# Splitting streamed weights 1024 columns at a time, into two wide pairs of tiles

## The chip, the cores and the metric

The kernel runs on one core of one Trainium2 chip. The metric is the device time of one execution in microseconds (us). Lower is better. The kernel before has a median of 2492.58 us over three runs (2488.17 to 2494.41).

## The reference

Two layers of a decoder trunk on 512 tokens of width 1024, all in float32. Each layer computes, from the RMS-normed input, one wide input projection whose columns feed three branches, merges the branches by gates, and adds a feed-forward:

```python
def hybrid_layer(x, ...):
    xn = rmsnorm(x, norm1_g)
    proj = xn @ w_in                              # 1024 x 9568
    (ssd_z, ssd_xbc, ssd_dt, mla_cq, mla_ckv, mla_kr, gdn_qkv, gdn_z, gdn_b, gdn_a,
     gate_logits) = jnp.split(proj, split_at, axis=-1)
    y_ssd = ssd_mixer(ssd_z, ssd_xbc, ssd_dt, ...)           # conv, chunked scan, gated norm
    y_mla = mla_mixer(mla_cq, mla_ckv, mla_kr, cos, sin, ...)  # 8 heads, low-rank q and kv
    y_gdn = gdn_mixer(gdn_qkv, gdn_z, gdn_b, gdn_a, ...)     # conv, gated delta rule
    g_ssd, g_mla, g_gdn = jnp.split(jax.nn.sigmoid(gate_logits), 3, axis=-1)
    mixed = g_ssd * (y_ssd @ w_ssd_out) + g_mla * (y_mla @ w_mla_out) + g_gdn * (y_gdn @ w_gdn_out)
    h = x + mixed @ w_out
    f = jnp.square(jax.nn.relu(rmsnorm(h, norm2_g) @ w_up)) @ w_down    # 1024 -> 4096 -> 1024
    return h + f
```

A final RMSNorm follows the second layer.

## The kernel before, in words

Each dense product is computed from parts. A float32 operand is split into a high part (rounded to the reduced format `fp32r`) and a low part, the exact rest; a product is three matmuls, high x high, high x low and low x high (`mm3`, lines 182 to 184). Activations are split once and stay in SBUF (`xh`, `xl`, `yh`, `yl`, `fh`, `fl`, eight tiles of 128 x 512 each). Weights are streamed from HBM and split as they come.

The stream is the generator `weights` (lines 165 to 179). It brings 1024 columns per partition (512 KB) into a raw tile `wraw` of a ring of two, by one DMA on the SyncE queue: two rows of k-tiles of 512 columns, four of 256 or eight of 128. `split_half` (156 to 163) then splits each half, 512 columns: ScalarE copies `raw` to `whi` (line 161), VectorE subtracts `raw - whi` into `wlo` (line 162), both at high priority. `whi` and `wlo` come from the pool `wp`, a ring of four 512-column tiles each; a tile goes back to the ring when its last matmul is done. A caller may pass `hold`, a list of tiles of its own, where all the weights of a product must stay (the second half of the output projection and the last down projection of a layer).

Two functions consume the stream. `dense_F` (186 to 209) makes feature-major products: a weight tile is the stationary operand, 512 tokens move past it, one PSUM bank for each 128 columns of weights. `dense_T` (214 to 249) makes token-major products: an activation tile is stationary and the weights move, one PSUM bank for each of the four token tiles. `dense_F` is called with 256 columns nearly everywhere (gates and branch projections in `out_proj`, convolved channels, the up projection), so a piece of 512 columns is two k-tiles for two banks, 12 matmuls. With `dense_T` at 512 columns a piece is one k-tile for four banks, also 12. With `mid`, `dense_T` uses the first four pieces on half of the tokens before the other half of the norm is done.

In the latent attention (lines 532 to 645), for each of four pairs of heads, the query weights have a stream of their own (`q_weights`, 533 to 548): 384 columns of a k-tile at a time, reordered by two strided copies (544, 545) and two subtractions (546, 547), into the same rings `whi` and `wlo`. The key and value weights of the pair come next as a list: one raw tile, two pieces.

Each engine works through its instructions in an order that a scheduler of the language fixes when the program is built, from priorities and its own estimate of times. It interleaves stages: while the attention or the delta rule waits for a chain of small steps, matmuls of the next dense product stand between them on TensorE. The order of a layer is: query and key/value latents, attention with four pairs of heads, state-space branch in two groups, delta rule (blocks inverted on VectorE, lines 812 to 836; two units, 878 to 987), the three branch projections in between, output projection, feed-forward in four quarters.

Of the kernel before, what the change touches and what calls it, by code (L numbers as in the profile page):

```python
# [59 lines left out]
def hybrid_kernel(ctx, tc, a, out, depth=2, taps=None):  # L60
# [95 lines left out]
    def split_half(raw, hold=None):  # L156
        """The exact high and low parts of 512 columns (or fewer) of raw weights."""
        n = raw.shape[1]
        hi, lo = hold or (mk(wp, [P, n], F32R, "whi"), mk(wp, [P, n], F32R, "wlo"))
        with tc.high_priority():  # L160
            act.copy(hi, raw)  # L161
            dve.tensor_tensor(lo, raw, f32(hi), ALU.subtract)  # L162
        return hi, lo

    def weights(w2d, c0, n, K, hold=None):
        """Yields (k0, hi, lo): split rows of w2d's columns c0 .. c0 + n, some k-tiles at a time.

        hold: the pairs of tiles for 512 columns, where the working ring's are too few.
        """
        kt = min(1024 // n, K // P)  # L170
        step = 512 // n
        for k0 in range(0, K // P, kt):
            raw = mk(wp, [P, kt * n], F32, "wraw", 2)
            sync.dma_start(raw.rearrange("p (k n) -> p k n", n=n),
                           w2d[k0 * P : (k0 + kt) * P, c0 : c0 + n].rearrange("(k p) n -> p k n", p=P))
            for q in range(0, kt, step):
                hi, lo = split_half(raw[:, q * n : (q + step) * n], hold and hold[k0 + q])
                v = lambda x: x.rearrange("p (k n) -> p k n", n=n)
                yield k0 + q, v(hi), v(lo)
# [6 lines left out]
    def dense_F(gen, cols, K, xh, xl, mid=None):  # L186
        """Feature-major products; cols: the slices of the weights' columns, one PSUM bank each.

        mid: called between the two halves of the tokens, which are then computed one after the other.
        """  # L190
        pss = [acc_bank() for _ in cols]
        last = K // P - 1
        if mid:
            gen = list(gen)
            for i, hf in enumerate(HALVES):
                for ps, c in zip(pss, cols):
                    for k0, wh, wl in gen:
                        for k in range(wh.shape[1]):
                            kk = k0 + k
                            mm3(ps[:, hf], wh[:, k, c], wl[:, k, c], xh[kk][:, hf], xl[kk][:, hf], kk == 0, kk == last)  # L200
                if i == 0:
                    mid()
            return pss
        for k0, wh, wl in gen:
            for ps, c in zip(pss, cols):
                for k in range(wh.shape[1]):
                    a_, b_ = wh[:, k, c], wl[:, k, c]
                    mm3(ps[: a_.shape[1], :], a_, b_, xh[k0 + k], xl[k0 + k], k0 + k == 0, k0 + k == last)
        return pss
# [4 lines left out]
    def dense_T(gen, n, K, xh, xl, evac, cols=lambda w: w, mid=None, hook=None):  # L214
        """Token-major products of n columns, one token tile a PSUM bank.

        mid: called after the first weights' products of the first half of the tokens.
        hook: the weights are all held; tokens go tile by tile, hook(t) is called after each tile's.
        """
        pss = [acc_bank()[:, :n] for _ in range(T)]  # L220
        last = K // P - 1

        def part(w, ts):
            k0, wh, wl = w
            for t in ts:
                tok = slice(t * P, (t + 1) * P)
                for k in range(wh.shape[1]):
                    kk = k0 + k
                    mm3(pss[t], xh[kk][:, tok], xl[kk][:, tok], cols(wh[:, k, :]), cols(wl[:, k, :]), kk == 0, kk == last)

        if hook:
            gen = list(gen)
            for t in range(T):
                for w in gen:
                    part(w, (t,))
                evac(t, pss[t])
                hook(t)
            return
        if mid:
            lead = [next(gen) for _ in range(4)]  # L240
            for w in lead:
                part(w, (0, 1))
            mid()
            for w in lead:
                part(w, (2, 3))
        for w in gen:
            part(w, range(T))
        for t in range(T):
            evac(t, pss[t])
# [32 lines left out]
    def norm_half(i, xs, ssq, gcol, pl, hs, ls):  # L282
        """The normed rows' transposes, split, of half the tokens; xs: token tiles [P, D]."""
# [21 lines left out]
    def small_weights(ly):  # L305
        """The columns k_rope | dt | a | b of w_in."""
        raw = mk(wp, [P, KD * 96], F32, "wraw", 2)
        sync.dma_start(raw, a["w_small"][ly])
        res = []
        for q in range(2):  # L310
            hold = [mk(lp, [P, 384], F32R, "mix", 8) for _ in range(2)]
            hi, lo = split_half(raw[:, q * 384 : (q + 1) * 384], hold)
            res.append((4 * q, hi.rearrange("p (k n) -> p k n", k=4), lo.rearrange("p (k n) -> p k n", k=4)))
        return res
# [17 lines left out]
    for ly in range(depth):  # L332
# [40 lines left out]
        def step_sizes():  # L373
            """Softplus of dt and alpha, decays, beta."""
            # softplus of dt and alpha: max(v, 0) + log1p(exp(-|v|))
# [43 lines left out]
        def cum_rows(pl):  # L419
            """Of each token tile's running sums of g: W [row, t, m] and M [row, t, i, l], such that the product over  # L420
            the rows of one group of four heads is the difference of the sums at l and at m of its head i.

            Rows 0 .. 63 pair ones with the sums' high and low parts at l, rows 64 .. 127 the negated parts at m
            with ones.
            """
# [26 lines left out]
        def seg_exp(pl, o, t, h0):  # L452
            """o[m, i, l] = exp(min(sum of g over m < k <= l, 0)) of heads h0 .. h0 + 3, for m <= l; else at most 1."""
# [27 lines left out]
        def latent(tok, width, gi, nm):  # L481
            """RMS-normed latent rows, transposed and split."""
# [22 lines left out]
        def rope(src):  # L505
            """Rotary embedding of the rows of src [P, S], two heads of 64 features."""
# [25 lines left out]
        for hp in range(4):  # L532
            def q_weights():
                for k0 in (0, 2):
# [3 lines left out]
                    for k in range(2):  # L538
                        rv = raw[:, k * 384 : (k + 1) * 384].rearrange("p (h n) -> p h n", h=2)
                        hi = mk(wp, [P, 384], F32R, "whi")  # L540
                        lo = mk(wp, [P, 384], F32R, "wlo")
# [27 lines left out]
            # each head's high part on both halves of the partitions, against the key's high and low parts  # L569
# [21 lines left out]
            for j in range(2):  # L591
# [26 lines left out]
                for kbs in ((0,), (1,), (3, 2)):  # L618
# [11 lines left out]
                    else:  # L630
                        # the first block of columns stays zero
# [18 lines left out]
        def conv_silu(pl, ps, taps_, bias, o):  # L650
            """o = 2 * silu(causal depthwise conv of the rows of ps)."""
# [10 lines left out]
        def silu_T(pl, c0, o):  # L662
            """o[P, T, 512] = 2 * silu of the token-major projection's 512 columns at c0."""
            dense_T(weights(w_in, c0, 512, D), 512, D, xh, xl, lambda t, ps: silu2(o[:, t, :], ps))
# [98 lines left out]
        def key_tiles(c0):  # L763
            """Two key-head tiles of q or k after the convolution."""
# [5 lines left out]
        def gdn_matrix(u):  # L770
            """Per chunk and head, the transpose of -strict(k k^T * decay) * beta."""
# [4 lines left out]
            for t in range(T):  # L776
# [5 lines left out]
                for i in range(2):  # L782
                    # the diagonal holds the squared lengths
# [28 lines left out]
        def gdn_blocks():  # L812
            """The inverses of I minus the 32 x 32 diagonal blocks, one a partition: forward substitution.

            Returns per unit the inverses and their transposes, rows on the partitions of their blocks.
            """
# [21 lines left out]
        def gdn_inverse(nt, xc, yc):  # L838
            """The transposed inverse of I - transpose(nt), by doubling of the diagonal blocks."""
# [38 lines left out]
        def gdn_unit(u, kT, ork, cc, cd, Yt, yh, yl):  # L878
# [35 lines left out]
            for t in range(T):  # L914
# [54 lines left out]
                # q's norm and its 128 ** -0.5 scale the rows of o  # L969
# [68 lines left out]
        def finish(t):  # L1038
            """After the layer's last product of a token tile."""
# [45 lines left out]
def lay_out(inputs):  # L1085
    """The launch's arrays: small parameters side by side, the narrow columns of w_in gathered."""
# [26 lines left out]
```

## Time and profile before

| | |
|---|---|
| median of three runs | 2492.58 us (2488.17 to 2494.41) |
| span of the profiled execution, first to last instruction | 2476.9 us |
| TensorE matmul (PE) busy | 2433.8 us, 98% |
| VectorE (DVE) busy | 1434.1 us, 58% |
| ScalarE (ACT) busy | 1049.5 us, 42% |
| GpSimd (POOL) busy | 54.2 us, 2% |
| copies of line 161 into `whi`, 128x512 | 664, 620 ns each |
| subtractions of line 162 into `wlo`, 128x512 | 664, 689 ns each |
| DMA | 215.17 MB, mean 87 GB/s |

The page gives the profiled execution by its span alone; its own time with what lies around the span isn't shown. PE counts an interval as busy while any matmul is under way, and matmuls overlap, so two starts lie closer together than one matmul lasts. In the rows of the groups the name `acc<-xh,whi` reads: written to `acc`, moving operand `xh`, stationary operand `whi`. The times in a row are the total busy time and the mean of one instruction, then the idle time of its engine just before, with what ended it.

### The profile page before, as it was taken

What the parts mean: (1) busy time and instruction counts of PE and PEld (TensorE: products, weight loads), DVE (VectorE), ACT (ScalarE), POOL (GpSimd) and SP (SyncE); (2) the same over time, 40 slices, a digit from 0 to 9 for tenths busy, and PEclk for the clock granted to TensorE, in tenths of its full rate; (3) what the DMA queues carried; (4) which work ended last, traced back from release to release, by engine and by line L of the source; (5) the groups of instructions that cost most, each with busy time, mean ns of one, the idle gap of its engine ahead of it and who ended that gap; (6) DMA issues with size and microseconds to landing.
All of it is one profiled execution on the core that took longest, in us unless ns stands there. A gap on an engine that the chain in (4) does not pass through costs nothing. (4 is left out here: it accounts for less than half of the span.)

```text
span 2476.9 us, 32227 instructions
## 1 busy us (share of the span) xinstructions
PE 2433.8 (98%) x12164; PEld 1949.4 (79%) x12164; DVE 1434.1 (58%) x2952; ACT 1049.5 (42%) x2189; POOL 54.2 (2%) x70
## 2 busy tenths in 40 slices
PE   7999999999999999999999999999999999999998
PEld 6777787777787888888887777877787878888887
DVE  6776756765675553443557667667656645443444
ACT  5555434434543342332445553444434534422333
POOL 0000000000000000000000000000000000000000
PEclk9999999999999999999999999999999999999999
DMA  4222232342222413223422222223422224222222
GB/s 129 81 60 69 68 86 73 95 114 69 69 68 71 154 64 94 94 94 94 137 74 69 60 77 67 87 69 102 103 77 69 60 77 153 77 94 94 94 94 94
DMA packets 194683, 215.17 MB, mean 87 GB/s; under 512 B 32864, under 2 KB 154208, under 8 KB 194528
## 3 DMA queue, kind: packets, MB, share of 16 engines
q1 hardware_dynamic: 191008, 207.87, 28.2%
q10 hardware_dynamic: 3520, 5.25, 0.9%
q8 instruction: 95, 1.56, 0.3%
q14 instruction: 60, 0.49, 0.1%
HBM read 200.50 MB, written 7.34 MB: 84 GB/s over the span
## 5 line engine op out<-in xcount | busy, mean ns | idle before, releaser
L162 DVE TENSOR_TENSOR wlo<-wraw,whi 128x512 fp32r<-128x512 f32 x664 | 456.6, 689 | 609.2 <-ACT whi L161 598.9
L161 ACT CAST whi<-wraw 128x512 fp32r<-128x512 f32 x664 | 410.6, 620 | 866.4 <-PE acc L183 511.8
L182 PE MATMUL acc<-xh,whi 128*128 128x512 f32 (+1 forms) x1376 | 543.3, 395 | 2.2 <-DVE vl L254 2.2
L183 PE MATMUL acc<-xl,whi 128*128 128x512 f32 (+1 forms) x1376 | 541.3, 394 | 0.0
L184 PE MATMUL acc<-xh,wlo 128*128 128x512 f32 (+1 forms) x1376 | 540.7, 393 | 0.0
L182 PEld LDWEIGHTS acc<-xh,whi 128*128 128x128 f32 x1376 | 258.4, 188 | 58.8 <-DVE vl L254 2.8
L183 PEld LDWEIGHTS acc<-xl,whi 128*128 128x128 f32 x1376 | 258.5, 188 | 57.8 <-issue 1.0
L184 PEld LDWEIGHTS acc<-xh,wlo 128*128 128x128 f32 x1376 | 258.4, 188 | 56.1 <-issue 0.5
L183 PE MATMUL acc<-yl,whi 128*128 128x512 f32 x384 | 154.7, 403 | 0.0
L182 PE MATMUL acc<-yh,whi 128*128 128x512 f32 x384 | 154.4, 405 | 0.0
L184 PE MATMUL acc<-yh,wlo 128*128 128x512 f32 x384 | 154.0, 401 | 0.0
L184 PE MATMUL acc<-whi,xl 128*128 128x512 f32 (+1 forms) x384 | 145.7, 379 | 0.0
L182 PE MATMUL acc<-whi,xh 128*128 128x512 f32 (+1 forms) x384 | 144.8, 379 | 0.0
L183 PE MATMUL acc<-wlo,xh 128*128 128x512 f32 (+1 forms) x384 | 144.7, 377 | 0.0
L659 DVE SCALAR_TENSOR_TENSOR cva<-acc,pc,cva 128x511 f32<-128x511 f32 (+2 forms) x168 | 120.2, 743 | 17.3 <-ACT cva L655 9.9
L182 PE MATMUL acc<-whi,yh 128*128 128x512 f32 x320 | 126.6, 396 | 0.0
L183 PE MATMUL acc<-wlo,yh 128*128 128x512 f32 x320 | 126.6, 396 | 0.0
L184 PE MATMUL acc<-whi,yl 128*128 128x512 f32 x320 | 126.6, 396 | 0.0
L183 PEld LDWEIGHTS acc<-yl,whi 128*128 128x128 f32 x384 | 72.1, 188 | 18.0 <-issue 1.9
L182 PEld LDWEIGHTS acc<-yh,whi 128*128 128x128 f32 x384 | 71.5, 188 | 18.1 <-ACT yh L257 2.3
L184 PEld LDWEIGHTS acc<-yh,wlo 128*128 128x128 f32 x384 | 72.1, 188 | 17.1 <-issue 1.0
L182 PEld LDWEIGHTS acc<-whi,xh 128*128 128x128 f32 x384 | 72.4, 189 | 13.9 <-DVE cva L659 0.5
(335 smaller groups left out, 3912.8 us busy)
## 6 DMA issues: line engine op xcount, KB each, us to landing
wraw<-in_w_in_dram SPq DMA_DIRECT2D x148, 512.0 KB, 3.6
wraw<-in_w_up_dram SPq DMA_DIRECT2D x64, 512.0 KB, 3.6
wraw<-in_w_down_dram SPq DMA_DIRECT2D x64, 512.0 KB, 3.6
wraw<-in_w_mla_out_dram SPq DMA_DIRECT2D x16, 512.0 KB, 3.4
wraw<-in_w_ssd_out_dram SPq DMA_DIRECT2D x16, 512.0 KB, 3.4
wraw<-in_w_gdn_out_dram SPq DMA_DIRECT2D x16, 512.0 KB, 3.4
wraw<-in_w_out_dram SPq DMA_DIRECT2D x16, 512.0 KB, 3.7
wraw<-in_mla_w_uq_dram SPq DMA_DIRECT2D x16, 384.0 KB, 3.3
```

What stands on the lines that cost most here:

```text
L161: act.copy(hi, raw)
L162: dve.tensor_tensor(lo, raw, f32(hi), ALU.subtract)
L182: pe.matmul(o, ah, bh, start=start, stop=False)
L183: pe.matmul(o, ah, bl, start=False, stop=False)
L184: pe.matmul(o, al, bh, start=False, stop=stop)
L659: dve.scalar_tensor_tensor(acc[:, d:], ps[:, : S - d], taps_[3 - d], acc[:, d:], ALU.mult, ALU.add)
```

## The change

A streamed raw tile that is not held is now split whole: one copy and one subtraction of 1024 columns. The ring has two pairs of 1024-column tiles in place of four of 512, the same SBUF. A piece now holds two, four or eight k-tiles, so 24 matmuls. The query weights of the attention keep their pieces of 384 columns, and take them from the same ring, which has two slots now. The key and value weights are one piece. `dense_T` with `mid` takes two pieces ahead in place of four. Held weights are split by 512 as before. Comments and docstrings are gone, with no effect.

```diff
     def split_half(raw, hold=None):
         n = raw.shape[1]
-        hi, lo = hold or (mk(wp, [P, n], F32R, "whi"), mk(wp, [P, n], F32R, "wlo"))
+        hi, lo = hold or (mk(wp, [P, n], F32R, "whi", 2), mk(wp, [P, n], F32R, "wlo", 2))
         with tc.high_priority():
             act.copy(hi, raw)
             dve.tensor_tensor(lo, raw, f32(hi), ALU.subtract)
         return hi, lo
...
         kt = min(1024 // n, K // P)
-        step = 512 // n
+        step = max(512 // n, 1)
         for k0 in range(0, K // P, kt):
             raw = mk(wp, [P, kt * n], F32, "wraw", 2)
             sync.dma_start(raw.rearrange("p (k n) -> p k n", n=n),
                            w2d[k0 * P : (k0 + kt) * P, c0 : c0 + n].rearrange("(k p) n -> p k n", p=P))
+            v = lambda x: x.rearrange("p (k n) -> p k n", n=n)
+            if not hold:
+                hi, lo = split_half(raw)
+                yield k0, v(hi), v(lo)
+                continue
             for q in range(0, kt, step):
-                hi, lo = split_half(raw[:, q * n : (q + step) * n], hold and hold[k0 + q])
-                v = lambda x: x.rearrange("p (k n) -> p k n", n=n)
+                hi, lo = split_half(raw[:, q * n : (q + step) * n], hold[k0 + q])
                 yield k0 + q, v(hi), v(lo)
...
         if mid:
-            lead = [next(gen) for _ in range(4)]
+            lead = [next(gen) for _ in range(2)]
...
             def q_weights():
...
-                        hi = mk(wp, [P, 384], F32R, "whi")
-                        lo = mk(wp, [P, 384], F32R, "wlo")
+                        hi = mk(wp, [P, 384], F32R, "whi", 2)
+                        lo = mk(wp, [P, 384], F32R, "wlo", 2)
```

## The prediction

> **What bounds the kernel now.** I read the page's busy times first, then the windows by stage.
>
> ```profile
> span 2476.9 us, 32227 instructions
> PE 2433.8 (98%) x12164; PEld 1949.4 (79%) x12164; DVE 1434.1 (58%) x2952; ACT 1049.5 (42%) x2189; POOL 54.2 (2%) x70
> ```
>
> ```profile
> core 0: us, PE busy (x) PEld busy (x) DVE busy (x) ACT busy (x) POOL busy (x), PEclk, DMA share, GB/s
> 0.00:62.00 62.00, 49.10 (x290) 42.39 (x291) 38.03 (x93) 36.62 (x87) 4.88 (x15) 1.00 0.43 129
> 62.00:124.00 62.00, 58.65 (x307) 45.91 (x306) 46.43 (x118) 36.62 (x99) 1.01 (x1) 1.00 0.29 81
> 124.00:186.00 62.00, 59.30 (x311) 45.49 (x310) 43.39 (x107) 33.66 (x90) 0.00 (x0) 0.97 0.22 60
> 186.00:930.00 744.00, 739.16 (x3841) 590.56 (x3840) 465.51 (x974) 324.86 (x661) 20.78 (x21) 1.00 0.29 83
> 930.00:1178.00 248.00, 248.00 (x1065) 199.45 (x1064) 101.02 (x155) 76.69 (x130) 0.00 (x0) 1.00 0.30 94
> 1178.00:1302.00 124.00, 122.72 (x633) 102.41 (x632) 64.06 (x132) 55.46 (x127) 4.52 (x8) 1.00 0.33 105
> 1302.00:1426.00 124.00, 118.50 (x614) 90.88 (x612) 85.27 (x216) 68.50 (x184) 0.00 (x0) 0.97 0.24 64
> 1426.00:2418.00 992.00, 986.54 (x4892) 790.42 (x4891) 564.76 (x1118) 400.52 (x783) 20.78 (x21) 1.00 0.30 87
> 2418.00:2477.00 59.00, 51.88 (x225) 41.88 (x224) 25.59 (x45) 16.55 (x36) 2.19 (x4) 0.97 0.26 94
> ```
>
> TensorE (PE) is the bound: 2476.9 - 2433.8 = 43.1 us of the span are not PE. Of these 62 - 49.10 = 12.9 lie in the first window and 59 - 51.88 = 7.1 in the last, where inputs arrive and the output leaves. The other 23 us sit mostly in the latent attention (3.35 + 2.70 in layer 0, 1.28 + 5.50 around it in layer 1). In the feed-forward window 930:1178 PE never idles, and 248.00 / 1065 = 0.233 us is the spacing of its 512-column matmuls. So the change, which shortens ACT and DVE work, can gain at most a part of those 23 us; it can lose wherever a split weight piece now comes late.
>
> Next, what a split costs and when it starts (rows of the groups, shapes apart, then of the waits):
>
> ```profile
> L162 DVE TENSOR_TENSOR wlo<-wraw,whi 128x512 fp32r<-128x512 f32 x664 | 456.6, 689 | 609.2 <-ACT whi L161 598.9 <-PE acc L184 5.6 <-PE sm L686 2.3
> L161 ACT CAST whi<-wraw 128x512 fp32r<-128x512 f32 x664 | 410.6, 620 | 866.4 <-PE acc L183 511.8 <-PE acc L184 315.9 <-DVE tok L826 9.8
> L546 DVE TENSOR_TENSOR wlo<-wraw,whi 128x256 fp32r<-128x256 f32 x32 | 13.4, 419 | 6.2 <-ACT whi L544 6.2
> L544 ACT CAST whi<-wraw 128x256 fp32r<-128x256 f32 x32 | 13.1, 409 | 6.9 <-PE acc L184 5.0 <-PE acc L183 1.1 <-DMA wraw<-in_mla_w_uq_dram 0.5
> L547 DVE TENSOR_TENSOR wlo<-wraw,whi 128x128 fp32r<-128x128 f32 x32 | 9.1, 284 | 0.0
> L545 ACT CAST whi<-wraw 128x128 fp32r<-128x128 f32 x32 | 9.8, 306 | 0.0
> L288 DVE TENSOR_SCALAR xr<-h,nrs 128x1024 f32<-128x1024 f32 x16 | 12.1, 758 | 7.6 <-POOL nrs L262 7.1 <-DMA wraw<-in_w_small_dram 0.4
> ```
>
> ```profile
> ACT whi L161 <- PE acc L183: 511.8, 331, 5.7
> ACT whi L161 <- PE acc L184: 315.9, 157, 3.8
> ```
>
> The copies stand ready and wait for PE to give a slot back (488 of 664 times). The ring is full, and its depth decides how early a piece is ready.
>
> **The change part by part.**
>
> *Fewer, wider splits.* 664 copies and 664 subtractions become 332 of each, 1024 columns wide. No such copy is in the trace. From 256 to 512 columns ACT grows by 0.211 us and DVE by 0.270, so 1024 columns are estimated at 0.620 + 0.422 = 1.04 us on ACT and 0.689 + 0.540 = 1.23 on DVE. Bounds for the subtraction are 0.758 (the one 1024-column DVE row, another operation) and 2 x 0.689 = 1.38; I take 1.23, from the same operation. ACT saves 332 x (1.24 - 1.04) = 66 us, DVE 332 x (1.38 - 1.23) = 49. Both lie beside PE work, so I count them as nothing by themselves. The Trainium skill (Perfetto Trace Analysis, Optimizing Scalar/DVE Operations) gives about 93 ns of access overhead an instruction for ScalarE and 60 for VectorE, by which the savings would be an estimated 31 and 20 us. The same section says that larger operations help an engine that is saturated, and that where an unsaturated one causes bubbles elsewhere, breaking its instructions up lets work finish sooner: this speaks against the change, and DVE's 58% and ACT's 42% put the kernel in its second case.
>
> *A ring of two wide pairs, in the dense stages.* In the feed-forward one old piece feeds 12 matmuls, a wide one 24. An old piece goes into a slot that becomes free three pieces before it is needed, 36 x 0.233 = 8.4 us; a wide one has a single piece, 24 x 0.233 = 5.6 us. What the split takes out of that:
>
> ```profile
> 1001.61 0.62 ACT L161 CAST whi<-wraw 128x512 fp32r<-128x512 f32 x1 [1.93 <-PE acc L183]
> 1002.27 0.69 DVE L162 TENSOR_TENSOR wlo<-wraw,whi 128x512 fp32r<-128x512 f32 x1 [1.78 <-ACT whi L161]
> ```
>
> Copy start to end of subtraction is 1.35 us, so pieces lie ready 8.4 - 1.35 = 7.0 us ahead. After: 1.04 + 1.23 + 0.04 between them = 2.3, so 5.6 - 2.3 = 3.3 us ahead. That is halved but still positive: cost 0. The cover is 3.3 us; what is queued in front on ACT and DVE may take that long and no more. In the built order of the changed program half of the wide pieces have 5.8 us of matmuls or more between the release and the first use, and nine in ten have about 5 or more.
>
> *The query weights of latent attention.* Their pieces are 384 columns, but now share the two slots where there were four. This is the costly edit. One piece feeds 9 matmuls = 2.1 us. Before, all four pieces of a unit of two heads could be split ahead; in the built order no release lay less than 3.9 us of matmuls before the use. Now pieces three and four and the key/value piece behind them (one wide piece, 2.3 us of splitting) each wait for a release about one piece ahead: covers of 0.2 to 3 us are common there. The split itself takes 0.409 + 0.419 + 0.284 = 1.11 us, and other work stands between:
>
> ```profile
> 97.38 0.41 ACT L544 CAST whi<-wraw 128x256 fp32r<-128x256 f32 x1 [0.58 <-PE acc L183]
> 97.69 0.58 ACT L253 CAST kh<-acc 128x512 fp32r<-128x512 f32 x1
> 98.17 0.30 ACT L545 CAST whi<-wraw 128x128 fp32r<-128x128 f32 x1
> ```
>
> With one such operation (0.58) ahead on ACT and a 0.69 one on DVE a piece needs 2.4 us against 2.1: a stall of 0.3. With two more it is 1.5; with none, zero. There are three such waits in each of 4 units x 2 layers = 24. Bounds: 0 and 24 x 1.5 = 36 us. I take 0.5 each, 12 us, and put a third of it into time in which PE idles anyway (the attention windows hold 12.8 us of idle): +8. Behind a waiting copy on ACT stand the exponentials and evictions of the running head, and behind the subtraction the row maxima; PE's next score product waits for them, so a stall is not repaid at once. The raw tiles are freed by these splits too, so SP issues the next query DMA later:
>
> ```profile
> wraw<-in_mla_w_uq_dram SPq DMA_DIRECT2D x16, 384.0 KB, 3.3
> ```
>
> It lands 3.3 us after its issue, inside one attention unit, so this costs nothing unless two splits in a row are late.
>
> *End of the delta rule.* In the built order the first two gate pieces of the last branch projection have their copy on ACT behind work that waits for a matmul only 0.3 to 0.4 us before the first use (3.5 us before the change). The low part is needed after 1.2 and 1.5 us and takes 2.3: 1.1 + 0.8 in each layer, 3.8 us; I take +3, as PE waits there already in part (idle of 4.84 and 5.46 in the long windows).
>
> *Start.* The first query-latent piece is 0.42 longer on ACT and 0.54 on DVE, with PE waiting: +1.
>
> *Earlier banks.* With twice the columns a piece, the first bank of a product ends 12 matmuls before the second in place of 6, and token tiles end six matmuls apart in place of three; evictions and the latent norms start up to 1.4 us sooner. Where PE waits for those, it gains; -1 a layer, -2.
>
> *Nothing.* Held weights (output projection's second half, last down projection) keep their 512-column splits; the lead of two wide pieces in the first product holds the same four k-tiles; semaphores fall in number beside full PE time.
>
> Sum: 8 + 3 + 1 - 2 = +10 us on a span of 2476.9, 2486.9. The page gives no time beyond its span; the median of the runs shown, 2492.6, lies 15.7 us above the span, which I keep: **2503 us**. The change of 0.4% is little above the 0.3% (7.5 us) that a measurement of this kernel can tell from no change.
>
> **The rivals.**
>
> *Faster: relief wins.* 115 us less ACT and DVE work reaches PE where the chains are latency-bound, in the attention windows (DVE 46.43 of 62) and the delta rule. It can take no more than the 23 us of inner idle; if a third goes, and the query pieces find their engines free (zero stalls), -8: 2485. It decides if PE's idle in 62:186 falls below the 6.05 us of now. Against it: that idle is mostly of transfers and of chains with few splits in them.
>
> *No change.* Query stalls fall into gaps already there: 0 to +5, about 2495.
>
> *Slower: convolutions use up the lead.*
>
> ```profile
> L659 DVE SCALAR_TENSOR_TENSOR cva<-acc,pc,cva 128x511 f32<-128x511 f32 x56 | 41.6, 745 | 16.5 <-ACT cva L655 9.9 <-ACT cva L657 6.6
> L266 DVE SCALAR_TENSOR_TENSOR ft<-ft,cva 128x512 f32<-128x512 f32 x56 | 38.2, 688 | 9.4 <-ACT ft L265 8.4
> ```
>
> Each tile brings 3 x 0.745 + 0.688 = 2.9 us to DVE, two tiles 5.8, at the same priority as the splits. If both stand before a subtraction, 5.8 - 3.3 = 2.5 us are lost, 28 pairs of tiles x 2.5 = 70 at worst; at a half, with the rest, 2503 + 35 = 2538. For it: the lead of 7.0 us covered this, 3.3 does not. Against: the split comes at high priority as well, between the tiles.
>
> *Slower: the clock.* The granted clock is 0.97 in 124:186 and in 1302:1426, the two windows with attention's long waits: 0.03 x 62 = 1.9 and 0.03 x 124 = 3.7 us. If the new stalls join old waits into long ones in four more units, at 1.9 to 3.7 each, that is about +11: 2514. The Trainium skill (TensorE: Matmul & The Clock Gate, Why this matters for your kernels) says that an idle window of some 3 us halves the clock; the trace agrees as far as the clock falls only where waits are longest.
>
> **How the numbers follow.** The forecast has 0.43, no change 0.22, faster 0.18, convolutions 0.10, clock 0.07. Of the forecast's own spread (+3 to +25) about 0.05 falls inside 0.3%. So faster 0.18, same 0.27, slower 0.55. The range reaches from the faster case, 2484, over the upper bound of the query stalls with the delta rule (+36 + 1) to 2530; the convolutions at full price and a few microseconds of the faster side are left out.
>
> **What would show it.** Right: 332 copies near 1.04 us and as many subtractions near 1.23; PE idle in the attention windows up by some 4 us a layer, with `acc` matmuls of the query latents waiting for ACT or DVE; 930:1178 still without idle; about 2 us more idle at the end of the delta rule. Wrong: idle in the feed-forward or the convolution stages (the lead is smaller than 3.3), or attention windows with less idle than now (relief), or subtractions far from 1.23.

## The result, and the profile after

The changed kernel takes 2507.0 us in the median (11 runs, 2504.3 to 2513.6), the kernel before 2489.1 beside it (11 runs, 2470.8 to 2505.6): a ratio of 1.0085, 95% interval 1.0061 to 1.0109, slower by 15 to 27 us. (This ratio is not the quotient of the two medians, which is 1.0072.) The profiled execution took 2506.3 us, 1.8 more than its span.

The page after, span and busy times, then the groups of the splits (out<-in, count | busy us, mean ns of one | idle before and what ended it):

```profile
span 2504.5 us, 31169 instructions
...
PE 2447.0 (98%) x12164; PEld 1952.8 (78%) x12164; DVE 1407.5 (56%) x2620; ACT 996.1 (40%) x1857; POOL 54.2 (2%) x70
```

```profile
L162 DVE TENSOR_TENSOR wlo<-wraw,whi 128x1024 fp32r<-128x1024 f32 x332 | 406.2, 1224 | 536.1 <-ACT whi L161 533.6 <-PE acc L186 1.0
```

```profile
L161 ACT CAST whi<-wraw 128x1024 fp32r<-128x1024 f32 x332 | 348.5, 1050 | 734.9 <-PE acc L187 401.4 <-PE acc L188 316.4 <-DMA wraw<-in_w_up_dram 6.9
```

The splits are what was forecast: 332 copies of 1.05 us and 332 subtractions of 1.22. ACT and DVE are less busy by 53 and 27 us, and the kernel is slower.

TensorE's own waits say where (waiting line <- what it waited for: us in total, times, longest); first the changed kernel, then the kernel before, whose lines have numbers lower by four:

```profile
PE sm L608 <- ACT qps L583: 11.4, 6, 3.3
...
PE sm L939 <- DVE tok L936: 4.0, 8, 0.8
PE sm L461 <- DVE sg L459: 3.6, 2, 1.8
...
PE acc L186 <- ACT whi L548: 3.0, 4, 0.9
...
PE acc L186 <- ACT whi L161: 2.1, 2, 1.1
```

```profile
PE sm L604 <- ACT qps L579: 4.6, 4, 2.1
...
PE sm L935 <- DVE tok L932: 1.3, 4, 0.3
```

TensorE hardly waits for a split: 5.1 us, the last two rows. What grew most is the wait of the first rope score product of a pair of heads (L608, L604 before) for `qps`, the rotated query, whose two halves are swapped by a DMA just before ("the swap" below).

The windows by stage show the same (start:end, length, then busy us of PE, PEld, DVE, ACT, POOL, the granted clock, DMA). Both kernels are cut at the same work, to within 0.6 us: the latent attention of a layer from its first rope product to its last value product, then what lies from there to the end of the delta rule ("the middle" below). Before, then after:

```profile
88.50:209.60 121.10, 117.80 (x614) 89.52 (x614) 83.32 (x212) 67.32 (x178) 0.52 (x1) 0.99 0.21 58
209.60:772.20 562.60, 557.98 (x2985) 444.20 (x2983) 373.77 (x807) 251.01 (x513) 18.05 (x16) 1.00 0.29 79
1313.00:1436.90 123.90, 119.56 (x616) 90.47 (x615) 83.19 (x212) 67.68 (x179) 0.52 (x1) 0.97 0.21 57
1436.90:2000.10 563.20, 557.93 (x2984) 444.17 (x2983) 373.82 (x806) 251.02 (x513) 18.05 (x16) 1.00 0.28 79
```

```profile
87.80:220.50 132.70, 125.87 (x625) 94.34 (x625) 84.95 (x210) 67.01 (x175) 0.52 (x1) 0.92 0.21 56
220.50:789.00 568.50, 561.26 (x2987) 445.78 (x2986) 366.78 (x728) 236.66 (x435) 18.04 (x16) 1.00 0.28 78
1330.00:1461.20 131.20, 122.38 (x623) 92.32 (x623) 84.53 (x209) 66.44 (x173) 0.52 (x1) 0.95 0.21 57
1461.20:2028.80 567.60, 559.74 (x2987) 444.67 (x2986) 366.59 (x727) 236.61 (x435) 18.04 (x16) 1.00 0.28 78
```

The attention is longer by 11.6 and 7.3 us (8 in the second layer when it is cut at the products themselves), the middle by 5.9 and 4.4; everything else together is 1.6 shorter. In the attention PE's busy time grew too, by 8.1 and 2.8 us for 11 and 7 matmuls more: the granted clock is 0.92 and 0.95 there, against 0.99 and 0.97.

**Why the clock has to be taken out first.** The two profiled executions differ in their mean granted clock:

```profile
core 0: 2476.9 us, clock 0.997
```

```profile
core 0: 2504.5 us, clock 0.992
```

Each run comes with its span and mean clock. Over 93 runs of the kernel before, clock from 0.981 to 0.998 and span from 2471.4 to 2509.9, the two go together (correlation -0.99): 2.1 us for each 0.001, and 2.0 in the 29 runs beside the first experiments. A microsecond at half clock thus costs about 0.4 (0.5 / 2490 of the mean, times 2000). Below, "at full clock" is the span less 2.0 us for each 0.001 that its clock falls short of 1, averaged over the runs of a kernel (scatter 0.9 to 2.0). The kernel before stands at 2470.9 (2470.5 and 2471.4 beside later experiments) with a mean clock of 0.991 to 0.992, the changed kernel at 2487.7 with 0.991. So 17 us of the difference are not the clock and 0 to 2 are. Of the 27.6 us between the profiles 10 are: the profile of before was one of its runs with the highest clock.

### The profile page after: what moved, and what is told of

Its sections match the earlier page's. It is cut to its first block, busy times and chain, and to the rows that moved or that the text cites. A ratio compares the mean times of both kernels' runs of the same rounds, so it can differ in the third digit from the quotient of the medians.

```text
span 2504.5 us, 31169 instructions
## 1 busy us (share of the span) xinstructions
PE 2447.0 (98%) x12164; PEld 1952.8 (78%) x12164; DVE 1407.5 (56%) x2620; ACT 996.1 (40%) x1857; POOL 54.2 (2%) x70
## 5 line engine op out<-in xcount | busy, mean ns | idle before, releaser
L162 DVE TENSOR_TENSOR wlo<-wraw,whi 128x1024 fp32r<-128x1024 f32 x332 | 406.2, 1224 | 536.1 <-ACT whi L161 533.6
L161 ACT CAST whi<-wraw 128x1024 fp32r<-128x1024 f32 x332 | 348.5, 1050 | 734.9 <-PE acc L187 401.4
```

## The experiments

Times are medians of 12 runs (11 of the changed kernel, 29 to 35 of the one before), with the ratio to the kernel before in the same session; e11 and e12 are single runs.

| kernel | us | ratio, 95% interval | mean clock | at full clock |
|---|---|---|---|---|
| before | 2487.4 to 2490.3 | 1 | 0.991 to 0.992 | 2470.5 to 2471.4 |
| changed | 2507.0 | 1.0085, 1.0061 to 1.0109 | 0.991 | 2487.7 |
| e1, query k-tiles in pairs | 2489.9 | 1.0011, 0.9981 to 1.0040 | 0.994 | 2476.5 |
| e2, changed, splits of 512 | 2504.5 | 1.0050, 1.0022 to 1.0078 | 0.990 | 2483.3 |
| e3, before, two slots for query high parts | 2495.5 | 1.0010, 0.9978 to 1.0042 | 0.992 | 2475.1 |
| e4, changed, no swap | 2493.7 | 1.0020, 0.9992 to 1.0047 | 0.993 | 2478.7 |
| e5, before, no swap | 2496.9 | 1.0036, 1.0009 to 1.0064 | 0.990 | 2475.8 |
| e6, e1 with splits of 512 | 2489.2 | 1.0006, 0.9985 to 1.0027 | 0.993 | 2473.8 |
| e7, e1 with the swap on SyncE | 2480.6 | 0.9974, 0.9951 to 0.9996 | 0.996 | 2471.1 |
| e8, changed, swap on SyncE | 2499.3 | 1.0039, 1.0006 to 1.0073 | 0.993 | 2483.6 |
| e9, before, swap on SyncE | 2484.1 | 0.9977, 0.9949 to 1.0005 | 0.993 | 2467.2 |
| e10, e6 with the swap on SyncE | 2481.9 | 0.9959, 0.9932 to 0.9986 | 0.994 | 2467.2 |
| e11, changed, 3 subtractions in the feed-forward | 2521.2 | | 0.991 | |
| e12, changed, 4 subtractions there | 2587.8 | | 0.983 | |

The first theory was A: with two slots in place of four, the query pieces of the next pair of heads come late; fewer of their matmuls stand ahead of the first rope product, and TensorE waits there. The trace has 29, 30, 35 and 33 matmuls between the last score product of line 603 and the first of line 604 in the four pairs before, and 21, 21, 27 and 32 after. The rival B was the width: a 1024-column subtraction ends later everywhere.

**e1: both k-tiles of a raw tile of query weights in one wide pair.**

```diff
+                    hi = mk(wp, [P, 768], F32R, "whi", 2)
+                    lo = mk(wp, [P, 768], F32R, "wlo", 2)
                     for k in range(2):
-                        hi = mk(wp, [P, 384], F32R, "whi", 2)
-                        lo = mk(wp, [P, 384], F32R, "wlo", 2)
...                      (the same copies and subtractions, into columns k * 384 ..)
-                        yield k0 + k, hi.unsqueeze(1), lo.unsqueeze(1)
+                    yield k0, hi.rearrange("p (k n) -> p k n", k=2), lo.rearrange("p (k n) -> p k n", k=2)
```

> The changed kernel, except that both k-tiles of a raw tile of query weights go into one wide pair (768 of its 1024 columns), so that two pieces hold all four k-tiles of two heads. Theory A (query pieces): in the changed kernel only 21 query matmuls of the next two heads stand between the last k-part score product and the first rope score product of a pair of heads, where the kernel before had 29 to 33 matmuls, because the third and fourth piece wait for a slot; TensorE then waits for the rope chain (the row PE sm <- ACT qps) and the clock is halved behind that wait. With the paired pieces 25 to 32 stand there again. A expects a loss of no more than 8 us against the kernel before (about 2488 to 2497), at most two half-clock stretches in the attention, and attention stages of 122 to 126 us in place of 132.7 and 131.2. Theory B (width: the later end of a 1024-column split costs the time everywhere): the query pieces matter little, 2500 to 2510.

2489.9 us, where A had 2488 to 2497. At full clock 11.2 us of the 17 are back. 25, 32, 31 and 32 matmuls stand ahead of the rope products, and their wait has nearly gone:

```profile
PE sm L608 <- ACT qps L583: 0.9, 3, 0.5
```

**e2: the wide ring, filled by two copies and two subtractions of 512.**

```diff
-            act.copy(hi, raw)
-            dve.tensor_tensor(lo, raw, f32(hi), ALU.subtract)
+            for c in range(0, n, 512):
+                s = slice(c, min(c + 512, n))
+                act.copy(hi[:, s], raw[:, s])
+                dve.tensor_tensor(lo[:, s], raw[:, s], f32(hi[:, s]), ALU.subtract)
```

> The changed kernel, except that a wide tile is filled by two copies and two subtractions of 512 columns in place of one of each; ring and slots are those of the change. Theory A (slots of the query weights): the ring is unchanged, so the query matmuls ahead of the rope products stay at 21 and the loss stays: 2500 to 2510, attention stages of 129 to 134 us, four or more half-clock stretches in them. Theory B (width): with the old width of operations the loss goes, 2485 to 2495. Both expect ACT and DVE busy times back near those before (about 1049 and 1434 us).

The loss stays, 2504.5, as A had it and against B as the whole cause. Four half-clock stretches stand in its attention, whose stages (127.8 and 126.5 us) are a little under A's 129 to 134. Yet 4.4 us at full clock go with the width: a smaller share, but one that the prediction had put at nothing.

**e3: the kernel before, with two slots for the high parts of the query pieces.**

```diff
-                        hi = mk(wp, [P, 384], F32R, "whi")
+                        hi = mk(ml, [P, 384], F32R, "qwh", 2)
```

> The kernel before, except that the high parts of the query pieces come from a ring of two of their own; all splits stay 512 columns wide, streams keep four slots. Theory A: the third and fourth query piece again wait for a slot; 21, 23 and 30 matmuls stand ahead of the rope products in the three units with a next pair, so two of three units per layer lose as in the changed kernel: 8 to 16 us more than the kernel before (2497 to 2505), two half-clock stretches more in the attention. Theory B (width): no wide split, no loss: within 5 us of the kernel before.

A miss for A in this form. 21, 23, 30 and 33 matmuls stand ahead, nearly as few as after the change, but the ratio is 1.0010 and the loss at full clock 4 us, not 8 to 16. (The medians lie 8 us apart, and the interval reaches to 10; the 4 us are within B's 5.) TensorE does not wait for `qps` in the first two pairs of a layer at all. The timelines of the second pair of heads tell why (start, length, engine, line, what; in brackets the wait before it). The kernel before:

```profile
115.11 1.15 ACTq L572 DMA_DIRECT2D mix<-mix  x2
...
115.52 3.42 SPq L536 DMA_DIRECT2D wraw<-in_mla_w_uq_dram  x2
...
120.06 0.61 ACT L579 CAST qps<-mix 64x512 fp32r<-64x512 f32 x1 [0.44 <-DMA mix<-mix]
...
120.73 0.38 PE L604 MATMUL sm<-kps,qps 128*128 128x256 f32 x1 [0.55 <-ACT qps L579]
```

The changed kernel:

```profile
115.48 1.15 ACTq L576 DMA_DIRECT2D mix<-mix  x2
...
115.91 0.37 SPq L174 DMA_DIRECT2D wraw<-in_mla_w_ukv_dram  x1
...
118.94 0.50 PE L186 MATMUL acc<-cqh,whi 128*128 128x512 f32 x1 [0.89 <-ACT whi L548]
...
121.00 0.61 ACT L583 CAST qps<-mix 64x512 fp32r<-64x512 f32 x1 [2.12 <-DMA mix<-mix]
...
121.67 0.58 PE L608 MATMUL sm<-kps,qps 128*128 128x256 f32 x1 [1.76 <-ACT qps L583]
```

And e3:

```profile
118.82 1.15 ACTq L572 DMA_DIRECT2D mix<-mix  x2
...
122.25 0.62 ACT L579 CAST qps<-mix 64x512 fp32r<-64x512 f32 x1
...
123.09 0.28 PE L604 MATMUL sm<-kps,qps 128*128 128x256 f32 x1
```

In the first two a weight transfer starts 0.4 us after the swap is issued, and the copy that needs the swap runs 5 us (before) and 5.5 us (after) behind the issue. In e3 no weight transfer is near, and it runs 3.4 us behind, without a wait. The swap is two transfers of 128 KB, and the rope product needs both. From issue to landing they take, in these stretches of the kernel before, the changed kernel and e3:

```profile
DMA to landing us min/median/max: 2.3/3.4/4.4
```

```profile
DMA to landing us min/median/max: 2.4/3.7/5.0
```

```profile
DMA to landing us min/median/max: 2.2/2.3/2.3
```

So theory C: the loss in the attention is the landing of the swap against the matmuls ahead of the rope product. Before, 30 matmuls (7.0 us at 0.233) covered even a swap that met a weight transfer, but for 0.6 us; 21 (4.9 us) do not, and do cover one that lands alone. The swap is hardly later after the change: beside weight transfers, in the second and third pair of a layer, its later half lands in 4.4 to 6.4 us before and 4.9 to 6.3 after. What the change took away is cover. The Trainium skill (DMA: Bandwidth & Descriptors, Rules for kernel authors) says that DMAs issued from several engines run on the same 16 DMA engines and interleave; the trace agrees with its 4.4 and 5.0 us beside a weight transfer against 2.3 without one.

That accounts for 8.3 of the 11.4 us of waits. The other 3.1 are the fourth pair of each layer, where 32 matmuls stand ahead (33 before) and the swap lands in 2.3 us with no weight transfer beside it. There only 3.2 us of matmuls are left when the swap is issued, and a wide copy stands on ScalarE between the two copies that need the swap:

```profile
190.44 1.15 ACTq L576 DMA_DIRECT2D mix<-mix  x2
...
192.92 0.62 ACT L583 CAST qps<-mix 64x512 fp32r<-64x512 f32 x1
193.44 1.04 ACT L161 CAST whi<-wraw 128x1024 fp32r<-128x1024 f32 x1
194.51 0.61 ACT L583 CAST qps<-mix 64x512 fp32r<-64x512 f32 x1
...
195.18 0.38 PE L608 MATMUL sm<-kps,qps 128*128 128x256 f32 x1 [1.53 <-ACT qps L583]
```

In e1 the same wide copy stands in the same place without a wait: there 5.6 us lie between the issue of the swap and the rope product. So the cover that counts is what is left when the swap is issued, and the number of matmuls behind line 603 does not always tell it; a wide copy in the way adds to what must be covered.

**e4 and e5: the changed kernel and the one before, without the swap** (the copies read the other half in place).

```diff
-            qd = mk(lp, [P, S], F32, "mix", 8)
-            for i in range(2):
-                act.dma_start(qd[64 * i : 64 * i + 64], qr[64 * (1 - i) : 64 * (1 - i) + 64])
...
-                act.copy(qps[j][other], qd[other])
+                act.copy(qps[j][other], qr[other])
```

> The changed kernel without the transfer that swaps the halves of the rotated query (two DMAs on ScalarE's queue for each pair of heads); the copies read the rows of their own partitions instead, so the rope scores are of other rows. Theory C (cover against landing): what the change loses in the attention is the wait of the first rope score product for this transfer (PE sm <- ACT qps, 11.4 us), since fewer query matmuls stand ahead of it and the transfer lands 4.7 to 6 us after its issue where a weight transfer starts beside it, in place of 2.6 alone. C expects the wait under 1 us, the attention stages at 121 to 125 us in place of 132.7 and 131.2, and the time 2490 to 2497, 4 to 10 us above the kernel before without the swap. Theory D (late splits hold up the query matmuls themselves): the swap is beside the point, 2500 to 2508, 14 us or more above the kernel before without the swap.

> The kernel before without the same transfer; the other half of the comparison. Both theories: it loses its own waits on the rope products (4.6 us) and what of the half clock follows them, 2478 to 2487.

The changed kernel did what C expects: 2493.7, a wait for `qps` of 0.2 us in all, and attention stages of 118.1 and 119.5 us, a little under C's 121 to 125. The kernel before did not get faster: 2496.9 against 2478 to 2487, a miss for both theories. Without the swap the scheduler puts the rope products after 13 (e4) and 15 (e5) query matmuls, and in e5 after none at all in the fourth pair of a layer. There they wait for ScalarE, 4.8 us in each layer:

```profile
PE sm L601 <- ACT qps L576: 9.9, 3, 4.8
```

So e5 is no price of the swap, and no clean partner for e4. The distance of the two, 3 us at full clock (in the medians e4 is 3 us below e5), falls short of C's 4 to 10. As far as e5 can be used, it speaks against the 14 or more of D (late splits hold up the query matmuls themselves).

**e6: paired query tiles with splits of 512** (the edits of e1 and e2 together).

> The kernel with the query k-tiles in pairs (two slots hold all four), and each wide tile filled by two copies and two subtractions of 512 columns. At the same granted clock the paired kernel stands 6 us above the kernel before (2477 against 2471 with the clock full, by a line through the runs), with waits of 3.6 us for VectorE ahead of the running sums and 3.9 at the delta rule. If the width of the subtraction makes these (1.23 us in the way of short steps), they go here and the kernel is within 3 us of the one before at the same clock; if the order that the scheduler builds around two slots makes them, they stay and it is 5 to 8 above.

At full clock 2473.8, 2.7 under e1 and 3 above the kernel before. The two waits that were to go with the width stayed, as the order's effect would have it:

```profile
PE sm L941 <- DVE tok L938: 3.8, 8, 0.7
PE sm L463 <- DVE gcc L801: 3.5, 2, 1.8
```

They are L939 and L461 of the changed kernel. The 3 us that remain are at the edge of both expectations, so width and order each keep a share.

**e7, e8, e9 and e10: the swap on the SyncE queue,** in e1, the changed kernel, the kernel before and e6. There it is issued in one order with the weight transfers.

```diff
-                act.dma_start(qd[64 * i : 64 * i + 64], qr[64 * (1 - i) : 64 * (1 - i) + 64])
+                sync.dma_start(qd[64 * i : 64 * i + 64], qr[64 * (1 - i) : 64 * (1 - i) + 64])
```

> The kernel with the query k-tiles in pairs, and the swap transfer issued on the SyncE queue, behind or ahead of the weight transfers in one order, in place of ScalarE's queue. If two queues sharing the DMA engines are what makes the swap late, it lands in 2.6 to 3.5 us and no rope product waits; ScalarE also saves the 1.15 us of issuing it, 8 times. Expected: 2478 to 2490, at best 5 us under the paired kernel. The rival: SyncE stands at a weight transfer that waits for its raw tile when the swap is due, the swap is issued late, and the rope products wait longer: 2495 to 2510.

> The changed kernel with one edit: the swap transfer of the rotated query goes out on the SyncE queue. In the built order 25 and 29 query matmuls then stand ahead of the rope products, though the query pieces still have two slots. If the change's loss in the attention is cover against landing (theory C), it goes although the slots stay two: no wait of a rope product above 0.5 us, and the time falls from 2507 to 2485 to 2494. If the two slots themselves hold up the query matmuls (theory A in its first form), waits for whi stand in the attention and it stays at 2498 or above.

> The kernel before with the same edit. Theory C: the rope products of the kernel before waited 4.6 us in the profiled execution, and those waits go; at the same clock 3 to 5 us under the kernel before, 2478 to 2488. If it lands below the kernel with paired query tiles and this edit (2480.6), the wide splits are of no use of themselves.

> Paired query tiles, splits 512 columns wide into the wide ring, the swap on the SyncE queue. The narrow operations were worth 3 us at the same clock in the paired kernel (2473.8 against 2476.5) and 4 in the changed one (2483.3 against 2487.7). If width and swap are independent: 3 us under the paired kernel with this edit, 2475 to 2482. If what the narrow splits saved was the same wait as the one that the swap edit removes: no difference, 2479 to 2484.

The edit is worth 4 us at full clock in the changed kernel and in the one before, 5 to 7 with paired tiles. The swap lands in 2.2 to 2.8 us in e7, and no rope product waits. e7 and e10 are faster than both kernels of this study, e10 by 0.14 to 0.68% against the kernel before, e7 by so little that its interval just leaves 1 out; e9's interval still touches 1. At full clock e9 and e10 are level (2467.2), so the wide ring brings nothing of itself, and with splits of 1024 (e7, 2471.1) it loses 4 us. In the medians e9 (2484.1) stays above the mark of 2480.6 that its expectation had set, and e10 (2481.9) fits both of its own.

e8 came out at 2499.3, above the 2485 to 2494 of C and in the range that stood for theory A (2498 or above). TensorE waits for no query copy there, which A had asked for. But C's expectation that no rope product waits above 0.5 us was missed too:

```profile
PE sm L608 <- ACT qps L583: 2.7, 2, 2.2
```

The 2.2 us are the third pair of layer 1, where the later half of the swap took 4.0 us to land; why, is open. Otherwise its attention did what C says: 120.5 and 124.0 us, where the changed kernel has 131.9 and 131.0 and the kernel before 120.4 and 122.8 (cut at the last value product on a `mix` tile, up to 1 us ahead of the windows above). The queue is not all that differs: e8 has 25, 29, 29 and 32 matmuls ahead of its rope products, the changed kernel 21, 21, 27 and 32.

What stayed of e8's loss lies outside the attention. The scheduler moves up to 23 of the 512-column matmuls of a layer from one stage to another, so the stages are compared without them: length less 0.4 us for each us at half clock and less 0.232 us for each of these matmuls, of which every kernel here has 8592. Both layers together, one profile each:

| us | before | changed | e1 | e2 | e3 | e6 | e8 | e9 |
|---|---|---|---|---|---|---|---|---|
| attention | 127.3 | 132.8 | 126.4 | 131.5 | 127.2 | 125.7 | 128.1 | 123.8 |
| middle | 230.3 | 237.6 | 238.8 | 234.3 | 230.4 | 236.4 | 237.5 | 230.7 |
| the rest | 121.9 | 125.8 | 119.3 | 124.6 | 125.9 | 122.4 | 126.1 | 122.5 |

The change loses 5.5 us in the attention, 7.3 in the middle and 3.9 in the rest, 16.7 in all. The attention's part goes by pairing (e1, e6) and with the swap on the other queue (e8).

The rest, which ends with the latents and the query pieces of the first pair, loses 3 to 4 us in four kernels whose query pieces have two slots (changed, e2, e3, e8), and not where they are paired: that is what e8 keeps and e1 does not. e4, which has two slots and no swap, loses less than 1 us there by the same reckoning, so two slots alone do not settle it. Part of the rest is the start of the program, which differs by up to 3 us between these profiles; 2 to 2.5 of the 3 to 4 us lie between the two layers.

The middle loses 4 to 8 us wherever the ring has two wide slots, less with splits of 512 (e2 4.0, e6 6.1) than of 1024 (7.2 to 8.5), and nothing with four narrow ones (e3, e9). e10, e7 and e4 fit, with 4.8, 6.9 and 7.0.

**e11 and e12: more subtractions behind each streamed piece of the feed-forward,** to find the end of the lead.

```diff
+            for _ in range(3 if raw.shape[1] == 1024 and in_ff else 1):     # e12: 4
                 dve.tensor_tensor(lo, raw, f32(hi), ALU.subtract)
```

> The changed kernel with each subtraction of the feed-forward's streamed pieces issued three times in place of once (the same result, two more of 1.22 us behind each piece). By the prediction's sum a piece there lies ready 3.3 us before its use; the two more leave 5.6 - 1.05 - 3 x 1.22 = 0.9 us. If the sum of leads is right, TensorE still has no idle worth a microsecond in the feed-forward, and the stage is no longer than in the changed kernel. If the lead is smaller than it was summed (other work ahead on VectorE), each of some 60 pieces a layer loses part of 2.44 us: 20 us or more a layer.

> The changed kernel with each subtraction of the feed-forward's streamed pieces issued four times. Copy and four subtractions take 1.05 + 4 x 1.22 = 5.9 us, 0.3 more than the 5.6 that one piece's matmuls last, so that the lead of 3.3 us is used up. If that sum is the whole of it, each of some 58 streamed pieces a layer loses at least 0.3 us beyond the 9 that each feed-forward lost with three subtractions: 17 us or more a layer more, with waits of TensorE for wlo spread over the whole stage, where three subtractions left them at its first piece alone. If the ring gives more lead than was summed, no more than a few us are added.

The stretch 930 to 1178 of the feed-forward, PE busy first: after the change, in e11, and in e12:

```profile
930.00:1178.00 248.00, 248.00 (x1064) 199.45 (x1064) 96.38 (x110) 70.17 (x85) 0.00 (x0) 1.00 0.31 94
```

```profile
930.00:1178.00 248.00, 248.00 (x1062) 197.99 (x1061) 199.65 (x200) 69.19 (x85) 0.00 (x0) 1.00 0.30 94
```

```profile
930.00:1178.00 248.00, 239.75 (x991) 182.86 (x990) 229.84 (x225) 68.26 (x85) 0.00 (x0) 1.00 0.28 86
```

With 2.44 us more behind every piece TensorE still has no idle, with DVE busy 199.65 of 248 us; with 3.67 more it loses 8.25. From its first relu to the last square of its output (the first and last use of the tile `rl`) the feed-forward of the first layer takes 352.3, 361.1 and 387.1 us. e11's 9 us are one wait of 5.1 us at the first piece and a halved clock behind it, which the expectation (no idle worth a microsecond) had missed. e12 adds 26, 0.4 for each of about 60 pieces, within its expectation.

## Why the prediction was right, point by point

The forecast was 2503.0, the change +10 us. The median came out at 2507.0, 18 above the kernel before: inside the range, with the right sign, and 4 us off only because two errors went opposite ways: its base, the 2492.6 of three runs, was 3.5 us above the 2489.1 measured beside the changed kernel, and its change 8 us too small. That the distance is so small is luck.

- **Around the span: the wrong term.** 15.7 us were put around the span; there are 1.8 (2506.3 less 2504.5). What mainly separated the profile of before from its median was the clock, 0.997 in that run against a mean of 0.991 to 0.992.
- **Widths: right, priced too low.** 1.05 and 1.22 us were forecast as 1.04 and 1.23. Their cost was put at 0; e2 against the changed kernel and e6 against e1 show 4.4 and 2.7 us.
- **Ring in the dense stages: right.** The lead was put at 3.3 us. In the feed-forward after, two copies stand 5.60 us apart, as summed:

```profile
1006.13 1.05 ACT L161 CAST whi<-wraw 128x1024 fp32r<-128x1024 f32 x1 [2.04 <-PE acc L187]
1007.21 1.23 DVE L162 TENSOR_TENSOR wlo<-wraw,whi 128x1024 fp32r<-128x1024 f32 x1 [2.39 <-ACT whi L161]
1011.73 1.05 ACT L161 CAST whi<-wraw 128x1024 fp32r<-128x1024 f32 x1 [0.57 <-PE acc L187]
```

  The subtraction ends at 1008.44, 3.3 us before the next release, when its piece is due. e11 and e12 put the end of the lead between 2.44 and 3.67 us.
- **Query weights: right place, wrong wait, somewhat too small.** +8 was summed from 24 stalls of 0.5 us for the split. Waits for a query copy are 3.0 us in 4 cases, and 2.1 us in 2 cases are for the key/value piece that the same term held. PE's idle in the attention rose by 3.5 and 4.5 us a layer, as the sign of "some 4 us" had it, but most of it ahead of rope products and not of query matmuls. e1 shows 11 us for the query pieces, 6 in the attention and the rest ahead of it, by another way: the order of the matmuls changed, and the rope product no longer had enough of them ahead of it. The prediction counted matmuls between a slot's release and a piece's use, and not how many stand ahead of the next chain.
- **The raw tiles: not refuted, but a transfer was missing.** A query transfer issued later "costs nothing", it said. TensorE's listed waits show no cost of that by itself. The transfer that mattered is the swap, which the prediction didn't name: it lands late beside a weight transfer before the change as well as after (4.4 and 5.0 us in the second pair).
- **End of the delta rule: the term too small, by another wait.** +3 was for late gate pieces, and no wait of TensorE for one is listed: the 2.1 us of waits for a copy of line 161 are at `ckh`, the key and value products of the attention. The whole middle lost 7.3 us. The waits that grew there are for short VectorE steps, L939 by 2.7 us and L461 by 3.6. They stay with narrow splits (e6) and are absent with four slots, so the order built around two slots is the likelier cause of most of it, with the width behind 2 to 3 us (e2 against the changed kernel, e6 against e1). No run kept two slots with the old order, so this stays argued.
- **Start and earlier banks.** +1 and -2 were forecast. The first rope product comes 0.7 us earlier in layer 0, with eight 512-column matmuls (1.9 us) moved behind it; so neither can be read by itself.
- **The rivals.** Relief is out: PE's idle in the attention grew. The convolutions are out: TensorE has no wait for `wlo` of line 162 worth listing. The clock was rightly seen to fall behind joined waits in the attention: by the profiles its half-clock time rose from 10.2 to 34.2 us there, about 10 us of cost. But over the runs the mean clock differs by 0.001 at most, so the kernel before must lose about as much at other places in most of its runs; its one profile does not show where.

## What to carry to other kernels

A ring's depth sets more than whether a piece is ready: through the built order it sets how many independent matmuls stand ahead of each short chain, so count those that are left when the chain's transfer is issued, before and after, and hold them against the chain's latency with its transfers at their worst. Read a profile's mean clock next to that of the other runs before taking its span for the kernel's time. When a small tile shares a ring with large ones, fill the slot with several of them; when a small transfer on a chain meets large ones, try it on their queue.

## What the runs showed of the hardware

The clock was halved after 3.4 us in which TensorE had been busy about half of the time, with no gap of more than 2.2 us between two matmul starts; in the changed kernel, the stretch before and the one after:

```profile
117.40:120.80 3.40, 1.61 (x6) 0.67 (x4) 1.73 (x3) 1.46 (x3) 0.00 (x0) 1.00 0.62 188
120.80:127.60 6.80, 5.93 (x15) 3.63 (x15) 2.94 (x11) 3.11 (x10) 0.00 (x0) 0.50 0.05 6
```

The Trainium skill (TensorE: Matmul & The Clock Gate, Why this matters for your kernels) names idle gaps of more than some 3 us between bursts of matmuls as what drops the clock; here shorter ones did.

It was also halved with almost no idle. In e1, among the block inversions of the delta rule:

```profile
551.00:571.50 20.50, 20.42 (x269) 14.49 (x269) 7.28 (x16) 11.08 (x28) 0.00 (x0) 1.00 0.19 53
571.50:585.20 13.70, 13.70 (x69) 10.30 (x70) 2.66 (x5) 1.46 (x4) 0.00 (x0) 0.50 0.00 1
```

TensorE had been busy 20.42 of 20.50 us with 269 matmuls, 168 of them 32 x 32 ones, and then ran 13.7 us at half clock. Such stretches of 10 to 27 us stand at this place in the traces of e1, e3, e4, e5, e7, e9, e10, e11 and e12, and not in the two kernels' own profiles. What sets them off stays open. They may be part of the 39 us between the fastest and the slowest run of the kernel before; at 0.4 us each that would take about 98 us at half clock, and no profile here has more than 44 us of it in the middle.
